# Column halves in one group, an earlier read of one result and fewer warm-up products in a Strassen-type matmul with GELU

## The chip, the core and the metric

The kernel runs on one core of a Trainium2 chip. The metric is the device time of a whole execution in microseconds (us), the median of several runs. "Before" is the kernel without the change, "after" the kernel with it. Every run told here was in the fast state, with a granted TensorE clock of 0.999 or 1.000, except for three runs of e_order: they count as fast too, but had 0.998, which is taken up there. "Span" is the time from the first to the last instruction of a profiled run.

The engines: PE is TensorE (matmuls), PEld its weight loads, DVE is VectorE (element-wise sums, transposes), ACT is ScalarE (copies, GELU, squares), POOL is GpSimd (it issues the loads of the inputs), SP issues the output transfers. PE writes its sums to a memory of its own, PSUM, which is divided into banks.

## The reference

```
a, b: 4096 x 4096, float32
x = a @ b
out = 0.5 * x * (1 + tanh(sqrt(2 / pi) * (x + 0.044715 * x**3)))     # float32
```

## The kernel before

The operands are turned to 16 bits on their way in. Each matrix is cut into four quadrants, and the four quadrants of the result come out of seven products instead of eight (M1 to M7, with sums of quadrants as operands). The result is worked through in 16 groups; a group is one block of 512 x 512 in each quadrant of the result. The first group's first half of K is done by plain products, while the inputs come in ("load phase"). All later groups have 7 products x 4 steps x 16 matmuls.

```python
PRODUCTS = [
    ("M3", "Y", "11", ("12", "22", 1)),           # name, PSUM chain, operand of a, operand of b
    ("M5", "X", ("11", "12", -1), "22"),
    ("M7", "X", ("12", "22", -1), ("21", "22", 1)),
    ("M1", "X", ("11", "22", -1), ("11", "22", -1)),
    ("M4", "X", "22", ("21", "11", 1)),
    ("M2", "Y", ("22", "21", -1), "11"),
    ("M6", "Y", ("21", "11", -1), ("11", "12", 1)),
]
N_WARM = 46
AHEAD = 2
```

The sums are made on DVE two steps ahead of their use (`make_sums`, tiles aS and bS, three buffers each). A step is 16 matmuls of 512 columns: four row blocks i, four pieces j of K.

```python
    def products(acc, sa, sb, i, start, stop):
        ...
        for j in range(4):
            nc.tensor.matmul(
                acc[:, :], sa[:, j // 2, i * P : (i + 1) * P, j % 2], sb[:, j, :],
                start=start and j == 0, stop=stop and j == 3, skip_group_check=True,
            )

    def multiply(gi, s, q):
        name, chain = product(gi, s)[:2]
        first = q == 0 and name in ("M3", "M5")
        sa, sb = sums.pop((gi, s, q))
        for i in range(RT):
            acc = bank(gi, chain, i) if first else banks[chain, i]
            products(acc, sa, sb, i, first, q == QPH - 1)
            if q == QPH - 1:
                settle(gi, name, i)
```

`settle` combines the banks of PSUM when a product is complete. The ends of M2 (result C21) and of M6 (result C22) matter here. Each y has one of five buffers, which is free again when its output transfer has landed:

```python
    def new_y():
        return pool.tile([P, NC], F32, name="y", tag="y", bufs=5)
    ...
        elif name == "M2":
            y = new_y()
            tt(y, post.pop(("x1", i)), Y, ALU.subtract)     # reads the bank that M6 goes on to write
            if gi:
                flush()
            waiting.append((gi, i, 1, 0, y, y))
        elif name == "M6":
            y = new_y()
            tt(y, Y, post.pop(("x7", i)), ALU.add)
            flush()                                         # GELU and output of what waits
            waiting.append((gi, i, 1, 1, y, y))
```

The order in which DVE gets its work is that of the program:

```python
        for n, step in enumerate(steps):
            for fn, args in before.get(n, ()):
                fn(*args)                                   # loads, transposes, squares of this step
            if n + AHEAD < len(steps):
                gi, s, q = steps[n + AHEAD]
                if s >= 0:
                    make_sums(gi, s, q)
            if step[:2] != (0, 2):
                flush()
            combine()
            if step[1] < 0:
                plain(n)
            else:
                multiply(*step)
            if step == (0, 2, QPH - 1):
                flush()
```

## Time and profile before

| | before |
|---|---|
| median (range) of three runs | 1580.12 us (1579.08 to 1580.46) |
| span of the profiled run | 1577.1 us |
| PE busy | 1567.7 us, 7246 matmuls |
| DVE busy | 1233.7 us |
| PE starts: the first real product; the product that waits for b's transfer; M6 of the first group; third step of the second group | 14.37, 35.74, 113.72, 128.23 us |

PE is busy for 99% of the span, so what can be gained without taking matmuls away is the handful of gaps in the rest. A gap is found in the list of waits, and where it lies is found in the order of time. Two cautions on reading. A matmul's duration in the records (379 ns) is its latency; the cost is the distance between starts (216 ns). And a gap in the order of time counts from the modelled end of the matmul before; where I give a wait to 0.01 us, it is the distance between the two starts in the trace's records less 0.216, and comes out 0.16 us larger.

### The profile page before, as it was taken

The numbers are of one execution on the slowest core, as the hardware profiler recorded it, in microseconds if no ns is written. First come the engines' busy times: TensorE is split into PE (matmuls) and PEld (weight loads), VectorE is DVE, ScalarE is ACT, GpSimd is POOL, SyncE is SP. The second block draws the span as 40 slices with busy tenths as digits, with TensorE's granted clock in tenths as the row PEclk, the third lists the DMA queues.
The fourth block names the chain that finished last, engine by engine and source line by source line (L and its number), as shares of the span: only waits on it lengthen the run. The fifth ranks groups of instructions, "written<-read, shape, count | busy, mean of one in ns | idle before, by whom it ended". The sixth has DMA issues, their size and how long they took to land. (4 is left out here: it accounts for less than half of the span.)

```text
span 1577.1 us, 19678 instructions
## 1 busy us (share of the span) xinstructions
PE 1567.7 (99%) x7246; PEld 709.6 (45%) x7246; DVE 1233.7 (78%) x1381; ACT 518.0 (33%) x710; POOL 537.7 (34%) x980
## 2 busy tenths in 40 slices
PE   9999999999999999999999999999999999999998
PEld 4444444444444444444444444444444444444443
DVE  1698888967787888895778778887687778988775
ACT  1036445311122545531111344542211145364111
POOL 7753442420234144341124413245011443314400
PEclk9999999999999999999999999999999999999999
DMA  9999884882968378686597937679468885747802
GB/s 173 198 215 189 132 162 79 161 162 48 193 106 158 87 131 160 108 179 115 87 161 117 186 72 142 146 113 182 79 121 146 134 160 93 151 105 134 161 28 82
DMA packets 225047, 211.13 MB, mean 134 GB/s; under 512 B 20144, under 2 KB 192176, under 8 KB 224944
## 3 DMA queue, kind: packets, MB, share of 16 engines
q0 software_dynamic: 187648, 142.67, 61.7%
q1 hardware_dynamic: 37296, 67.13, 11.8%
q8 instruction: 59, 0.97, 0.2%
q14 instruction: 44, 0.36, 0.1%
HBM read 285.22 MB, written 67.11 MB: 223 GB/s over the span
## 5 line engine op out<-in xcount | busy, mean ns | idle before, releaser
L331 PEld LDWEIGHTS <-aS 128*128 128x128 f16 x4960 | 485.3, 98 | 587.2 <-issue 2.2
L186 POOL DMA_DIRECT2D bR<-in_b_dram x832 | 447.6, 544 | 700.0 <-DVE bS L302 329.7
L302 DVE TENSOR_TENSOR aS<-aT 128x2048 f16<-128x2048 f16 (+1 forms) x312 | 376.1, 1212 | 151.0 <-PE accX L331 114.5
L331 PE MATMUL accX<-bS,aS 128*128 128x512 f16 x1984 | 431.1, 379 | 0.0
L302 DVE TENSOR_TENSOR bS<-bR 128x2048 f16<-128x2048 f16 x310 | 376.1, 1218 | 69.3 <-PE accX L331 58.5
L331 PEld LDWEIGHTS <-aT 128*128 128x128 f16 x1984 | 194.2, 98 | 234.8 <-issue 0.8
L422 ACT ACTIVATE y<-y 128x512 f32<-128x512 f32 x192 | 118.5, 630 | 351.8 <-DVE y L431 351.4
L331 PE MATMUL accY<-bS,aS 128*128 128x512 f16 x992 | 216.7, 379 | 1.8 <-DVE y L431 1.8
L331 PE MATMUL accY<-bS,aT 128*128 128x512 f16 x992 | 216.9, 379 | 0.5 <-DVE bS L302 0.5
L331 PE MATMUL accX<-bS,aT 128*128 128x512 f16 x992 | 216.7, 379 | 0.0
L331 PE MATMUL accX<-bR,aS 128*128 128x512 f16 x992 | 216.7, 379 | 0.0
L331 PE MATMUL accY<-bR,aS 128*128 128x512 f16 x992 | 216.7, 379 | 0.0
L186 POOL DMA_DIRECT2D stage<-in_a_dram x144 | 89.9, 630 | 249.0 <-DVE aT L161 178.0
L431 DVE TENSOR_TENSOR energy<-energy,square 128x1024 bf16<-128x1024 bf16 x240 | 164.4, 685 | 9.5 <-ACT square L207 5.7
L395 ACT COPY x<-accX 128x512 f32<-128x512 f32 x128 | 74.9, 585 | 224.3 <-PE accX L331 224.3
L207 ACT ACTIVATE square<-aT 128x1024 bf16<-128x1024 f16 x120 | 123.4, 1051 | 70.6 <-DVE energy L431 70.2
L207 ACT ACTIVATE square<-bR 128x1024 bf16<-128x1024 f16 x120 | 123.0, 1050 | 62.5 <-DVE energy L431 60.5
L161 DVE STREAM_TRANSPOSE aT<-stage 128x2048 uint32<-128x2048 uint32 (+1 forms) x37 | 74.6, 2017 | 46.0 <-DMA stage<-in_a_dram 39.9
L395 ACT COPY m<-accX 128x512 f32<-128x512 f32 x60 | 34.7, 579 | 215.7 <-PE accX L331 213.6
L422 ACT ACTIVATE y<-accX 128x512 f32<-128x512 f32 x64 | 38.2, 597 | 100.1 <-PE accX L331 99.9
L431 DVE TENSOR_TENSOR x<-accX,x 128x512 f32<-128x512 f32 x64 | 44.0, 691 | 21.8 <-ACT y L422 19.1
L431 DVE TENSOR_TENSOR y<-accY,m 128x512 f32<-128x512 f32 x60 | 39.9, 687 | 12.5 <-ACT m L395 12.4
(38 smaller groups left out, 344.9 us busy)
## 6 DMA issues: line engine op xcount, KB each, us to landing
bR<-in_b_dram POOLq DMA_DIRECT2D x832, 128.0 KB, 5.2
out_dram<-y SPq DMA_DIRECT2D x256, 256.0 KB, 5.7
stage<-in_a_dram POOLq DMA_DIRECT2D x112, 256.0 KB, 6.8
stage<-in_a_dram POOLq DMA_DIRECT2D x32, 128.0 KB, 5.1
row<-seen_d SPq DMA_DIRECT2D x2, 1.5 KB, 4.2
seen_d<-seen SPq DMA_DIRECT2D x1, 3.0 KB, 7.4
```

Of the source, the lines that this page charges most:

```text
L161: nc.vector.transpose(dst[:, :, x, :], src[:, :, x, :])
L186: nc.gpsimd.dma_start(out=dst, in_=src)
L207: nc.scalar.activation(t[:, :], src, ACT.Square)
L302: nc.vector.tensor_tensor(out=x, in0=y, in1=z, op=ALU.add if o[2] > 0 else ALU.subtract)
L331: nc.tensor.matmul(acc[:, :], sa[:, j // 2, i * P : (i + 1) * P, j % 2], sb[:, j, :], start=start and j == 0, stop=stop and j == 3, skip_g ...
L395: nc.scalar.copy(out=t[:, :], in_=src[:, :])
L422: nc.scalar.activation(y[:, :], src[:, :], ACT.Gelu_apprx_tanh)
L431: nc.vector.tensor_tensor(out=o[:, :], in0=x[:, :], in1=y[:, :], op=op)
```

## The change

Its intent, as far as the code tells: the third group (`gi == 2`) is multiplied in column halves; the reads of C21 go ahead of M6's last operand sums on DVE, so that M6 need not wait for its banks; and seven warm-up products that only keep the clock up go.

```diff
--- before.py
+++ after.py
@@ -49,7 +49,7 @@
     ("22", "21", "12", True), ("22", "22", "22", True),
 ]
 N_PLAIN = 2 * len(PLAIN)
-N_WARM = 46
+N_WARM = 39
 
 
 SQUARE_MAX = 2.0**26
@@ -323,15 +323,17 @@
         banks[chain, i] = t
         return t
 
-    def products(acc, sa, sb, i, start, stop):
+    def products(acc, sa, sb, i, start, stop, parts=1):
 
         sa = sa.rearrange("p (jj m e) -> p jj m e", jj=2, e=2)
         sb = sb.rearrange("p (kt n) -> p kt n", n=NC)
-        for j in range(4):
-            nc.tensor.matmul(
-                acc[:, :], sa[:, j // 2, i * P : (i + 1) * P, j % 2], sb[:, j, :],
-                start=start and j == 0, stop=stop and j == 3, skip_group_check=True,
-            )
+        w = NC // parts
+        for n in range(0, NC, w):
+            for j in range(4):
+                nc.tensor.matmul(
+                    acc[:, n : n + w], sa[:, j // 2, i * P : (i + 1) * P, j % 2], sb[:, j, n : n + w],
+                    start=start and j == 0 and n == 0, stop=stop and j == 3, skip_group_check=True,
+                )
 
     def warm():
         z = pool.tile([P, NC], F16, name="zeros", tag="bS", bufs=AHEAD + 1)
@@ -386,7 +388,7 @@
         sa, sb = sums.pop((gi, s, q))
         for i in range(RT):
             acc = bank(gi, chain, i) if first else banks[chain, i]
-            products(acc, sa, sb, i, first, q == QPH - 1)
+            products(acc, sa, sb, i, first, q == QPH - 1, parts=1 + (gi == 2))
             if q == QPH - 1:
                 settle(gi, name, i)
 
@@ -577,6 +579,8 @@
     at(len(groups) - 1, 2, 2, answer)
     at(len(groups) - 1, 4, 0, read)
 
+    late = (0, NP - 1, QPH - 1)
+
     with tc.manual_schedule():
         warm()
         table = pool.tile([P, 1], F32, name="table", tag="table")
@@ -586,9 +590,9 @@
             for fn, args in before.get(n, ()):
                 fn(*args)
             if n + AHEAD < len(steps):
-                gi, s, q = steps[n + AHEAD]
-                if s >= 0:
-                    make_sums(gi, s, q)
+                ahead = steps[n + AHEAD]
+                if ahead[1] >= 0 and ahead != late:
+                    make_sums(*ahead)
             if step[:2] != (0, 2):
                 flush()
             combine()
@@ -598,6 +602,8 @@
                 multiply(*step)
             if step == (0, 2, QPH - 1):
                 flush()
+            if step == (0, NP - 2, QPH - 1):
+                make_sums(*late)
         flush()
     return said["value"]
```

## The prediction

> **What bounds the kernel now.** I read the page first, then the list of who waited for whom on the matmul engine, then the order of time around each of those waits.
>
> The page's share of busy time says that TensorE matters:
>
> ```profile
> PE 1567.7 (99%) x7246; PEld 709.6 (45%) x7246; DVE 1233.7 (78%) x1381; ACT 518.0 (33%) x710; POOL 537.7 (34%) x980
> ...
> L331 PE MATMUL accX<-bS,aS 128*128 128x512 f16 x1984 | 431.1, 379 | 0.0
> ```
>
> The 379 ns is a latency, not the cost: 1984 matmuls kept the engine busy for 431.1 us, about 217 ns each. The windows view gives the rate without the ramp (columns: stretch, its length, busy time and count, clock, DMA share, GB/s); the second line is the third group:
>
> ```profile
> 218.00:314.50 96.50, 96.50 (x449) 1.00 0.70 131
> 320.00:1500.00 1180.00, 1180.00 (x5469) 1.00 0.72 131
> ```
>
> 1180 / 5469 = 215.8 ns per matmul, at full clock with no gap (record by record the starts are 215 or 216 ns apart). A weight load takes 98 ns (the mean in the page's row of L331 LDWEIGHTS) and starts 2 ns after the matmul ahead of it, so it is hidden with some 118 ns to spare. Everything that PE waits for after the warm-up is three waits:
>
> ```profile
> PE accY L331 <- DVE y L431: 1.8, 1, 1.8
> PE accX L343 <- DVE table L583: 1.4, 1, 1.4
> PE accY L331 <- DVE bS L302: 0.5, 1, 0.5
> PE accY L362 <- DMA bR<-in_b_dram: 0.5, 1, 0.5
> ```
>
> The second of these four is the program's start. From 128.23 us to the end PE runs 6688 matmuls without a gap, so any change of PE time after 128.23 arrives at the end in full, and any change before it arrives only if the matmul at 128.23 moves.
>
> **What the Trainium skill says.** Four places bear on it.
> - TensorE: Matmul & The Clock Gate, section "Wait — 56ns, not 53.3ns?": back-to-back warm matmuls start N / 2.4 GHz plus about 2.5 ns apart, a fixed cost per matmul. For 512 columns that is 215.8, which is what the trace has. For 256 it gives 109.2 ns; no row here shows that width yet.
> - The same page, "Back-to-back issue gap": in streams of weight load and matmul, 128 columns sustained about 81 ns per pair. So a pair can go faster than 109. The same sentence gives 131 ns for 512 columns, which this trace contradicts.
> - The same page, "What's actually happening": the clock is halved after at least one idle window of about 3.4 us. The trace agrees at the start: matmuls 427 ns apart until 7.4 us, then 216; and the waits of up to 1.9 us later did not lower the clock.
> - Trainium Kernel Development and Optimization, "Key Constraints": transfers issued from SP, ACT and POOL run on the same 16 DMA engines and interleave. The trace agrees: around 118 us an output of 256 KB takes 5.4 us to land behind loads.
>
> **Part 1, the third group by halves.** The group has 28 steps of 16 matmuls, 448 of 512 columns. The change makes them 896 of 256 columns, each with its own weight load: the column loop is outside, so the same four weights are loaded twice. The columns streamed stay the same, so with the rate formula the cost is the fixed part alone: 448 x 2.5 = +1.1 us (448 x 215.8 = 96.7 us becomes 896 x 109.2 = 97.8 us). The room for the weight load shrinks from 118 ns to 109 - 100 = 9 ns, by the trace's own 98 ns and 2 ns offset. That still fits, and the 81 ns pair says that the real limit is lower. The group has no wait of PE on anything, and DVE was busy 83.3 of 96.5 us there, so a slightly slower PE meets no new wait. It is on the path in full.
>
> **Part 2, C21's sums.** In the first group M2 finishes C21's base in the Y banks, and M6 adds on to the same banks, so DVE must read each bank (y = x - accY) before M6 may write it. DVE's order was: M6's four operand sums, then the four reads. The PE rows, and the DVE rows behind them:
>
> ```profile
> 104.88 7.07 PE L331 MATMUL accY<-bR,aS 128*128 128x512 f16 x32
> 113.72 7.07 PE L331 MATMUL accY<-bS,aS 128*128 128x512 f16 x32 [1.77 <-DVE y L431]
> ```
> ```profile
> 110.72 1.22 DVE L302 TENSOR_TENSOR aS<-aT 128x2048 f16<-128x2048 f16 x1
> 111.85 1.22 DVE L302 TENSOR_TENSOR bS<-bR 128x2048 f16<-128x2048 f16 x1
> 112.99 2.48 DVE L431 TENSOR_TENSOR y<-x,accY 128x512 f32<-128x512 f32 x4
> 115.38 1.22 DVE L302 TENSOR_TENSOR bS<-bR 128x2048 f16<-128x2048 f16 x1
> 116.51 2.49 DVE L431 TENSOR_TENSOR y<-y,c 128x512 f32<-128x512 f32 x4
> 118.92 1.22 DVE L302 TENSOR_TENSOR bS<-bR 128x2048 f16<-128x2048 f16 x1
> 120.06 0.68 DVE L431 TENSOR_TENSOR y<-accY,x 128x512 f32<-128x512 f32 x1
> 123.45 0.69 DVE L431 TENSOR_TENSOR y<-accY,x 128x512 f32<-128x512 f32 x1 [2.71 <-DMA out_dram<-y]
> 124.81 0.69 DVE L431 TENSOR_TENSOR y<-accY,x 128x512 f32<-128x512 f32 x1 [0.67 <-ACT y L422]
> 126.36 0.69 DVE L431 TENSOR_TENSOR y<-accY,x 128x512 f32<-128x512 f32 x1 [0.85 <-DMA out_dram<-y]
> 126.96 1.22 DVE L302 TENSOR_TENSOR bS<-bR 128x2048 f16<-128x2048 f16 x1
> ```
>
> The change swaps the first two rows with the third. The reads then start at 110.72 and are through by 113.2; M6 can follow M2 at 111.79 (111.57, the start of M2's last matmul, plus 0.216). M6's second step is due 16 x 0.216 = 3.45 us later, at 115.24, and needs the sum that now ends at about 114.24 + 1.22 = 115.46. PE's starts trail such an end by 0.05 us here, so it begins at 115.51: a new wait of 0.27. M6 ends 16 matmuls later, at 118.96 instead of 120.62: 1.66 us earlier.
>
> But the four DVE instructions only change places. DVE had been busy without a break since before 108, so the row at 115.38 and all after it stay where they are. The next group's third step needs the sum at 126.96, which stands in DVE's queue behind four writes of y. Those wait for buffers of y, five in all, which come free when C21's own outputs have landed. Outputs are issued when the sums with c (116.51) and their activations are done, and these don't move. So the sum still ends at 128.18 and the matmul still starts at 128.23. PE now arrives at 118.96 + 2 x 3.45 = 125.87 and waits 2.36 us instead of 0.70. Waits before: 1.93 + 0.70 = 2.63 (2.147 and 0.917 between starts, less 0.216 each; the view has 1.77 and 0.54, which count a modelled end). After: 0.27 + 2.36 = 2.63. Net **0**.
>
> **Part 3, 39 warm products.** Seven warm matmuls less are 7 x 0.216 = 1.5 us of PE work, ending at 14.30 - 1.51 = 12.79 instead of 14.30. But the first real matmul needs its transposed tile (DVE, first half done at 13.0) and its piece of b, whose last transfer landed at 14.24; the weight load started at 14.34. It was data that set that time, not the warm products. Even if it moved, PE is stopped further on by a transfer that nothing in PE releases:
>
> ```profile
> 14.37 7.07 PE L362 MATMUL accY<-bR,aT 128*128 128x512 f16 x32
> ...
> 35.74 1.45 PE L362 MATMUL accY<-bR,aT 128*128 128x512 f16 x6 [0.49 <-DMA bR<-in_b_dram]
> ```
>
> So the idle time before the data grows by 1.5 us and the end gets nothing: **0**. The sum of the three parts is +1.1 us, 1580.1 + 1.1 = 1581.2.
>
> **Rivals.**
> 1. The M6 gain is kept. That needs the y buffers to come free earlier, which would take earlier landings of C21's outputs. Against it: their issue hangs on DVE's fixed order, and DMA is saturated there. If all of the 1.66 came through: 1581.2 - 1.7 = 1579.5.
> 2. Weight loads become the bound of the halves. For it: only 9 ns to spare by the 98 ns of the profile. The TensorE page's "Step-by-step: what each phase is for" also has about 62 ns per matmul in the sequencer with hardware decode off; if a weight load costs the same, a pair takes 124 ns, an estimate from that page. Then 896 x 124 = 111.1 us, +14.4, giving 1594.5. Fully serial, 109 + 98 = 207 ns a pair, it would be 185 us, +89. Against both: weight loads now start right after a matmul's start and are hidden, and the page's 81 ns pair.
> 3. A longer idle stretch drops the clock: 2.36 us at 125.87 or 1.5 us before 14.3. Below 3.4 us, so I don't expect it; one window at half clock costs at most 1.7 us, and in the start the transfer at 35.74 hides most of it.
>
> **Range and chances.** Runs of before lie within 1.4 us. I take 1578.6 as the low end (rival 1 with noise) and 1585.5 as the high end (a pair of 109.2 + 5 ns would add 4.5 us). Slower by 2% needs +31.6 us, that is 143 ns a pair; faster by 2% cannot come from under 3 us of waits. I give 0.01, 0.97 and 0.02.
>
> **What would show it.** In the changed profile: the third group's matmuls as 896 rows in about 97.8 us, starts 109 ns apart; M6 starting near 111.8; a wait of some 2.4 us on DVE's bS sum just before 128.2, and 2.6 us of waits in that region as before; the first real matmul still near 14.4 and the wait near 35.7 unchanged. It is wrong if starts in the third group are well above 110 ns, or if the matmul after the bS sum begins before 127.5.

## The result, and the profile after

| | before | after |
|---|---|---|
| median (range), 4 runs each | 1579.91 us (1579.08 to 1580.46) | 1580.11 us (1579.39 to 1580.56) |
| span of the profiled run | 1577.1 | 1578.4 |
| first real product | 14.37 | 13.95 |
| wait for b's transfer ends | 35.74 | 35.34 |
| M2 starts | 104.88 | 105.89 |
| M6 starts | 113.72 | 112.80 |
| third step of the next group starts | 128.23 | 128.25 |
| third group, from its first start to the next group's | 96.7 (448 x 215.8 ns) | 97.81 (896 matmuls) |
| start of the last matmul | 1571.50 | 1572.64 |

The ratio of after to before is 1.0002, 95% interval 0.9987 to 1.0017: the same. A ratio here is the mean time of one kernel's fast runs over that of the other's of the same rounds, so it is not quite the ratio of the medians that are quoted beside it. The predicted 1581.2 (+1.1 us) lies inside the interval, and so does no change at all; the times alone don't tell those apart, the traces and the experiments do. In the two traces the third step of the second group starts 0.02 us later than before and the last matmul 1.13 us later: the +1.1 lies behind 128.25.

From the page of after: the busy time and the largest group of matmuls. Its mean of 366 ns mixes the two widths.

```profile
PE 1566.9 (99%) x7687; PEld 752.4 (48%) x7687; DVE 1233.5 (78%) x1381; ACT 518.3 (33%) x710; POOL 539.3 (34%) x980
...
L333 PE MATMUL accX<-bS,aS 128*128 128x512 f16 (+1 forms) x2112 | 431.6, 366 | 1.1 <-DVE aS L302 0.7
```

There are 441 matmuls more (448 by the halves, less 7 warm ones), and PE is busy for 0.8 us less: the warm products' 1.5 us are gone, and 0.7 came again, by the halves for the most part (in the trace of the halves alone PE is busy for 0.3 us more than before, not 1.1: these sums of modelled ends are too coarse for a count). The windows view of after over the third group (stretch, its length, busy time and count, clock, DMA share, GB/s):

```profile
218.10:315.70 97.60, 97.60 (x896) 1.00 0.70 131
```

97.60 / 896 = 108.9 ns; by the records the starts are 109.17 ns apart and the group lasts 97.81 us. I had written 109.2 and 97.8.

All waits of PE in after (engine, what it was to do, whom it waited for; total us, times, longest):

```profile
PE accY L364 <- DMA bR<-in_b_dram: 2.3, 2, 1.8
PE accX L345 <- DVE table L587: 1.4, 1, 1.4
PE accY L333 <- DVE bS L302: 1.3, 2, 0.7
PE accX L333 <- DVE aS L302: 0.7, 1, 0.7
PE accX L333 <- ACT m L397: 0.4, 1, 0.4
```

The 1.8 us wait for y at M6 is gone. In its place there are a wait for data at the start, two for bS and two new ones for aS and m. Their places, from the order of time of after's PE (start, length, what, count, and the gap before it with who ended it), the start first:

```profile
13.95 7.07 PE L364 MATMUL accY<-bR,aT 128*128 128x512 f16 x32 [1.75 <-DMA bR<-in_b_dram]
```

```profile
35.34 7.07 PE L364 MATMUL accY<-bR,aT 128*128 128x512 f16 x32 [0.51 <-DMA bR<-in_b_dram]
...
85.03 1.47 PE L333 MATMUL accX<-bS,aS 128*128 128x512 f16 x6 [0.69 <-DVE aS L302]
86.90 12.25 PE L333 MATMUL accX<-bS,aS 128*128 128x512 f16 x56 [0.41 <-ACT m L397]
...
112.80 3.62 PE L333 MATMUL accY<-bS,aS 128*128 128x512 f16 x16
117.04 3.61 PE L333 MATMUL accY<-bS,aS 128*128 128x512 f16 x16 [0.63 <-DVE bS L302]
120.49 7.07 PE L333 MATMUL accY<-bS,aT 128*128 128x512 f16 x32
128.25 7.07 PE L333 MATMUL accY<-bS,aT 128*128 128x512 f16 x32 [0.68 <-DVE bS L302]
```

M6 starts right behind M2 (105.89 + 6.91 = 112.80), as the change wants. Its second half then waits, and two steps later PE waits again and starts where it did before. The waits at 85 and 87 us belong to the load phase: a piece of a landed later in this run, and they lie ahead of the first DVE instruction that the change moves. DVE behind M6, in after's order of time:

```profile
111.73 1.87 DVE L433 TENSOR_TENSOR y<-x,accY 128x512 f32<-128x512 f32 x3
114.03 0.69 DVE L433 TENSOR_TENSOR y<-x,accY 128x512 f32<-128x512 f32 x1 [0.43 <-DMA out_dram<-y]
114.64 1.22 DVE L302 TENSOR_TENSOR aS<-aT 128x2048 f16<-128x2048 f16 x1
115.77 2.35 DVE L302 TENSOR_TENSOR bS<-bR 128x2048 f16<-128x2048 f16 x2
...
126.37 0.69 DVE L433 TENSOR_TENSOR y<-accY,x 128x512 f32<-128x512 f32 x1 [1.01 <-DMA out_dram<-y]
126.98 1.21 DVE L302 TENSOR_TENSOR bS<-bR 128x2048 f16<-128x2048 f16 x1
```

The reads of C21 now stand first; the fourth meets a y buffer whose output has not landed (0.43 us). The last line is the sum that the third step of the next group waits for. It still stands behind the writes of y, and they still wait for output transfers. (The same rows of before are in the prediction.)

### The profile page after: what moved, and what is told of

It reads as the page before. It is cut to its first block, busy times and chain, and to the rows that moved or that the text cites. A ratio compares the mean times of both kernels' runs of the same rounds, so it can differ in the third digit from the quotient of the medians.

```text
span 1578.4 us, 20560 instructions
## 1 busy us (share of the span) xinstructions
PE 1566.9 (99%) x7687; PEld 752.4 (48%) x7687; DVE 1233.5 (78%) x1381; ACT 518.3 (33%) x710; POOL 539.3 (34%) x980
## 5 line engine op out<-in xcount | busy, mean ns | idle before, releaser
L333 PEld LDWEIGHTS <-aS 128*128 128x128 f16 x5280 | 516.6, 98 | 557.0 <-issue 1.6
L333 PE MATMUL accX<-bS,aS 128*128 128x512 f16 (+1 forms) x2112 | 431.6, 366 | 1.1 <-DVE aS L302 0.7
L333 PEld LDWEIGHTS <-aT 128*128 128x128 f16 x2112 | 206.7, 98 | 222.7 <-issue 1.0
L333 PE MATMUL accY<-bS,aT 128*128 128x512 f16 (+1 forms) x1056 | 217.0, 366 | 0.7 <-DVE bS L302 0.7
L333 PE MATMUL accY<-bS,aS 128*128 128x512 f16 (+1 forms) x1056 | 217.0, 366 | 0.6 <-DVE bS L302 0.6
L333 PE MATMUL accX<-bR,aS 128*128 128x512 f16 (+1 forms) x1056 | 216.9, 366 | 0.0
L333 PE MATMUL accX<-bS,aT 128*128 128x512 f16 (+1 forms) x1056 | 216.9, 366 | 0.0
L333 PE MATMUL accY<-bR,aS 128*128 128x512 f16 (+1 forms) x1056 | 216.9, 366 | 0.0
```

The costliest lines, as they stand in the source:

```text
L333: nc.tensor.matmul(acc[:, n : n + w], sa[:, j // 2, i * P : (i + 1) * P, j % 2], sb[:, j, n : n + w], start=start and j == 0 and n == 0, s ...
```

## The experiments

Each run is of its own kernel, beside runs of before on the same chip. The single runs of before ranged over 1577.27 to 1580.82 us in these sets, so a difference of 1 us is at the edge of what the times can tell, and I use the traces for it.

**The halves alone (e_half).** The change of `products` and its call as in the diff above, with 46 warm products and the old order.

> The third group's halves alone, 46 warm products, old order of sums. Theory (a fixed 2.5 ns per matmul, weight loads hidden, all of it behind the last wait of the matmul engine): the group takes 97.8 us instead of 96.7, and the end comes 1.1 us later; ratio about 1.0007. Rival (the changed kernel's halves are free or the front part gave something back, since its median moved by only 0.2 us): 0 to 0.3 us.

Measured: 1580.22 us median (1579.42 to 1580.97) beside 1579.13, ratio 1.0006, interval 0.9992 to 1.0019. In the trace the group lasts 97.81 us, starts 109.17 ns apart, no wait in it. The centre fits +1.1 us; the interval does not exclude the rival, so the next run makes the cost larger.

**The halves in fifteen groups (e_half_all).**

```diff
-            products(acc, sa, sb, i, first, q == QPH - 1, parts=1 + (gi == 2))
+            products(acc, sa, sb, i, first, q == QPH - 1, parts=1 + (gi > 0))
```

> Halves in all fifteen groups after the first, nothing else changed: the suspected cost fifteen times over. Theory: 15 x 448 x 2.5 ns = 16.8 us more, about 1596.8 us, ratio 1.0106, matmul starts 109.2 ns apart throughout. Rival (the small difference seen is noise and the halves cost nothing): ratio 1.000. Rival (halves burden weight loads or fetching of instructions when they go on for long): over 25 us.

Measured: 1595.5 us (1594.54 to 1596.42) beside 1579.13, ratio 1.0100, interval 1.0085 to 1.0115; 16.4 us by the medians, 1.09 us a group. The windows view of this run over the same long stretch as in the prediction:

```profile
320.00:1500.00 1180.00, 1180.00 (x10812) 1.00 0.72 131
```

1180 / 10812 = 109.1 ns, against 215.8 for a matmul of double width: 2 x 109.1 - 215.8 = 2.4 ns for each matmul more. The cost of the halves is settled: it is a fixed cost per matmul (a third width follows in the next run), it is on the path in full, and it does not grow over fifteen groups.

**Quarters in the third group (e_quarter).** This asks how near the halves were to the limit of weight loads. "The skill's 81 ns" is the figure of "Back-to-back issue gap" that the prediction names.

```diff
+            products(acc, sa, sb, i, first, q == QPH - 1, parts=1 + 3 * (gi == 2))
```

> Third group by column quarters of 128, 1792 matmuls and weight loads. It asks how much room the halves had. If only the fixed cost counts, 1792 x 55.8 ns = 100.0 us, 3.3 us more than before. If a weight load must end before its matmul (2 + 98 ns): 1792 x 100 = 179 us, 82 us more. With the skill's 81 ns a pair: 145 us, 48 us more. I expect the 81 ns, so about 1628 us; the halves' 109 would then have 28 ns to spare.

Measured: 1582.12 us (1581.84 to 1583.49) beside 1579.13, ratio 1.0017, interval 1.0001 to 1.0032. I expected about 1628 and was wrong. The third group in the windows view of this run:

```profile
219.10:318.90 99.80, 99.80 (x1790) 1.00 0.69 129
```

99.80 / 1790 = 55.8 ns a pair, with a weight load for every matmul. The group lasted 100.0 us by the records, 3.3 more than before, which is the fixed cost alone. The records of weight loads still say 98 ns each, and nearly every one starts 1 to 2 ns after the matmul ahead of it, so here their records overlap one another: 98 ns is a latency too. The 9 ns of room that I gave the halves, and the 28 ns, were both no measure of it.

**88 warm products (e_warm88).** `N_WARM = 88`, nothing else.

> 88 warm products instead of 46, nothing else changed: 42 x 0.216 = 9.07 us more work of the matmul engine before its first real product. Theory (three waits in the first group soak up a shift of the start): they have 0.65 + 1.93 + 0.70 = 3.3 us to give, so the end comes 5.8 us later, and those three waits are gone from the trace. Rival (the start is on the path): 9.1 us later. Rival (transfers released later by the shift put new waits in their place): over 7 us.

Measured: 1585.97 us (1585.75 to 1586.49) beside 1579.13, ratio 1.0041, interval 1.0026 to 1.0057: 6.8 us by the medians, between the theory and the first rival. The wait for b's transfer is gone from the trace, as expected. The other two are not:

```profile
121.52 7.07 PE L331 MATMUL accY<-bS,aS 128*128 128x512 f16 x32 [1.42 <-DVE y L431]
...
136.01 7.07 PE L331 MATMUL accY<-bS,aT 128*128 128x512 f16 x32 [0.52 <-DVE bS L302]
```

Both moved with PE (M6 from 113.72 to 121.52, the third step from 128.23 to 136.01). They are not fixed points in time: DVE is fed by PE, and when all of it is late the wait is late too. Only the wait at 35.7, which is for a transfer that PE does not release, soaks up a shift of the start. By this trace the first real product started 8.88 us later (23.25 against 14.37); 8.88 - 0.65 (that wait) - 0.08 (a small one of before at 85.9) - 0.37 (what the other two shrank by) = 7.78, and both the third step and the end of the span come 7.8 later than in before's profiled run. Why the medians give a microsecond less is not shown; other runs of before in this set were not traced.

**39 warm products alone (e_warm39).** `N_WARM = 39`.

> 39 warm products alone. Theory (data sets the start of the first real product, and the later waits soak up the rest): 0, within 0.3 us, the first real product still between 13.9 and 14.4 us. Rival (the start moves and reaches the end): up to 1.5 us faster. Rival (the gap before the first product brings the clock down): about 1 us slower or hidden by the waits.

Measured: 1578.36 us (1577.97 to 1579.01) beside 1578.96, ratio 0.9997, interval 0.9983 to 1.0010. The first rival at its full 1.5 us (0.9990) is inside the interval, so the trace must say: the first real product started at 13.19, outside what I expected, and the wait near 35 ended at 34.90. Starting 1.2 us earlier than before's profiled run went with 0.8 there. But runs with 46 warm products had this wait end anywhere from 34.71 to 36.61, and the clock stayed up (starts 216 ns apart from the first real product on). I read it as no effect that can be told from the spread of the loads; a gain of some tenths of a microsecond is not excluded. One thing the traces do show against the theory: in five of the nine traced runs with 46 warm products (e_half, e_quarter, e_order_b, e_first, e_defer) the first real product started 0.216 us after the last warm one, with no wait between them (13.50 to 14.26 us). There the warm products and not the data set its start.

**One warm product (e_warm0).** `N_WARM = 1`.

> One warm product instead of 46. Theory: the first real product starts at about 14 us as before, since data sets it, but at half clock: up to 16 matmuls 427 ns apart instead of 216, 3.4 us later at most. The wait for b's transfer near 35.7 gives back 0.65 us (up to 1.2 in a late run); the waits after it don't, as the run with 88 warm products showed. So 1.5 to 2.8 us slower, ratio 1.001 to 1.0018. Rival (the matmul engine has time to spare in the load phase): 0.

Measured: 1579.38 us (1579.09 to 1579.61) beside 1579.03, ratio 1.0002, interval 0.9987 to 1.0018. I expected 1.5 to 2.8 us and got 0.3. Only ten real products started 427 ns apart (the start of before has 14 such distances; with a distance of 381 ahead of them and one of 277 behind, 2.1 us were lost, not 3.4), the first started at 13.28 instead of 14, and no wait is left near 36: the products that wait there in the other runs start at 36.12, which is inside the range of those runs. In the profiled run the third step came at 129.23, 1.0 us later than in before's. So even 45 warm products less cost too little to tell from the spread by the times, and from 7 less I expect no more.

**The order of C21's sums alone (e_order, and again as e_order_b).**

```diff
-                if s >= 0:
+                if s >= 0 and (gi, s, q) != (0, 6, 3):
                     make_sums(gi, s, q)
...
+            if step == (0, 5, QPH - 1):
+                make_sums(0, 6, QPH - 1)
```

> The order of C21's sums alone. Theory (the matmul engine only arrives earlier at its next wait, the sum of the next group's third step, which stands behind four writes of y that wait for buffers): 0, within 0.4 us; the wait just before 128 us grows to about 2.4 us, unless the transfers of this run put it elsewhere. Rival (the 1.7 us gained at M6 reach the end): 1.7 us faster, ratio 0.9989.

Measured: 1580.74 us (1579.13 to 1581.05) beside 1578.96, ratio 1.0010, interval 0.9996 to 1.0024. The rival's 0.9989 is excluded. From the order of time of this run's PE:

```profile
112.45 7.35 PE L331 MATMUL accY<-bS,aS 128*128 128x512 f16 x32
119.63 7.07 PE L331 MATMUL accY<-bS,aT 128*128 128x512 f16 x32
128.61 7.07 PE L331 MATMUL accY<-bS,aT 128*128 128x512 f16 x32 [1.91 <-DVE bS L302]
```

M6 has 0.28 us of wait left inside it (0.27 predicted), and PE then waits 2.07 for the third sum instead of 0.70. The time itself looked slower (1.8 us by the medians, where I expected at most 0.4), so I ran the same kernel again.

> The same kernel as e_order, a second time, because its first timing (ratio 1.0010, interval 0.9996 to 1.0024) left open whether the order of C21's sums costs something of its own. Theory (it is worth nothing either way, and the first set was the spread of the load phase): a ratio within 0.9994 to 1.0006. Rival (reading C21 earlier meets output buffers that have not landed, and costs about 1 us): again 1.0005 to 1.0015. The waits before its third step should again sum to about 2.4 us from M6 on.

Measured: 1579.01 us (1578.32 to 1581.03) beside 1579.03, ratio 1.0005, interval 0.9992 to 1.0019. Here the loads came early (35.7 is 34.71 in this run), PE ran ahead, and the wait for the third sum was 3.15 us; with 0.27 in M6 that is 3.42 us, not the 2.4 that I expected. Neither set shows a cost or a gain clear of noise, and 1.0005 lies in the range of the theory and at the edge of the rival's.

What the two sets do show is two clusters: 1578.32 to 1579.13 us (four runs, both traced ones among them) and 1580.29 to 1581.05 (six runs). Three of the slower six, all of e_order, had a granted clock of 0.998. In all 13 traces kept, the clock, once up, was at half only behind the last matmul and for at most 3.0 us, which makes 0.999 of the span (1 - 0.5 x 3.0 / 1577 = 0.99905). To be shown as 0.998 it takes at least 0.0015 x 1577 / 0.5 = 4.7 us at half clock, so in these three runs the clock was very likely down somewhere else too. The longest stretch without a matmul behind the start is the one before the third step (3.36 us from start to start in e_order_b), so the prediction's rival 3 may hold there: a longer wait that brings the clock down, worth up to 1.7 us by its estimate. That is not shown: none of the slower six was traced, three of them had 0.999, and runs of before with 1.000 reach 1580.82 too. No run of after had under 0.999.

The sharper measure of the waits is the distance in the trace from M2's first matmul to the third step's first, which leaves the load phase out (without any wait it would be the two steps of M2, the two of M6 and two more, 6 x 3.45 = 20.7; all columns in us, the waits from the distances of starts):

| kernel | near 35.7 | M2 starts | waits in M6 | wait, 3rd step | M2 to 3rd step |
|---|---|---|---|---|---|
| before | 35.74 | 104.88 | 1.93 | 0.70 | 23.35 |
| e_half | 35.20 | 104.45 | 1.93 | 0.84 | 23.49 |
| e_warm39 | 34.90 | 104.08 | 1.93 | 0.87 | 23.52 |
| e_warm0 | 36.12 | 105.19 | 1.58 | 1.75 | 24.04 |
| e_warm88 | 43.97 | 113.03 | 1.58 | 0.68 | 22.98 |
| after | 35.34 | 105.89 | 0.79 | 0.85 | 22.35 |
| e_order | 35.25 | 105.54 | 0.28 | 2.07 | 23.07 |
| e_order_b | 34.71 | 103.87 | 0.27 | 3.15 | 24.14 |
| e_first | 34.94 | 104.20 | 1.94 | 0 | 22.66 |
| e_order_first | 36.18 | 105.24 | 0 | 0 (4th: 1.36) | 20.73 |
| e_defer | 35.45 | 104.80 | 0.27 | 0 | 20.99 |

With the old order of everything the last column is 22.98 to 24.04 (first five rows), with C21's reads moved and nothing else in the queue 22.35 to 24.14 (after, e_order, e_order_b). The order moves the wait; what it does to the sum is within the spread between runs of one kernel (23.07 and 24.14 for e_order). The last three rows are of the runs that follow.

**The third sum first (e_first).** The old order of C21's reads, but the sum for the third step of the next group is put ahead of the four writes of y.

```diff
             products(acc, sa, sb, i, first, q == QPH - 1)
-            if q == QPH - 1:
+            if q == QPH - 1 and (gi, name) != (0, "M6"):
                 settle(gi, name, i)
+        if q == QPH - 1 and (gi, name) == (0, "M6"):
+            make_sums(1, 0, 2)
+            for i in range(RT):
+                settle(gi, name, i)
...
-                if s >= 0:
+                if s >= 0 and (gi, s, q) != (1, 0, 2):
```

> Old order of C21's sums, but the sum of the next group's third step is issued ahead of the four writes of y that wait for buffers. Theory: that takes away the last wait, 0.7 us faster, and the wait at M6 stays 1.9 us. Rival (the sum is late for its operands or its buffer, not for its place in the queue): 0.

Measured: 1577.43 us (1577.12 to 1577.93) beside 1578.96, ratio 0.9990, interval 0.9976 to 1.0004; unclear by the times alone. In the trace the wait before the third step is gone, and the one at M6 is 1.94 as before. So the sum was late for its place in the queue, not for its operands or its buffer: it now starts at 120.15 us instead of 126.96.

**Both orders (e_order_first).** The edits of the last two together.

> Both: the changed order of C21's sums, and the next group's third sum ahead of the writes of y; no halves, 46 warm products. Theory (the two waits are in series and each alone hides the other's gain): up to 2.3 us faster than before, about 1577.7, with 0.3 us left of the waits at M6 and in the next group together; somewhat less in a run whose loads come late. Rival (DMA sets the pace up to here and puts the wait at another transfer): under 0.7 us.

Measured: 1577.07 us (1576.27 to 1578.85) beside 1578.96, ratio 0.9985, interval 0.9971 to 0.9999. By the times this is not clear of the sum alone (0.9990). By the traces, from M2's first matmul to the fourth step's, it takes 25.5 us here (20.73 + 3.45 + 1.36), 26.1 in e_first and 25.8, 26.5 and 27.6 in the three traces with the new order of C21's reads and the old place of the third sum (after, e_order, e_order_b). So both edits together gain little more than one, in the profiled run at least, which was the slowest of the five:

```profile
119.06 10.52 PE L331 MATMUL accY<-bS,aT 128*128 128x512 f16 x48
130.77 3.61 PE L331 MATMUL accY<-bS,aT 128*128 128x512 f16 x16 [1.19 <-DVE bS L302]
```

Three steps now run through (x48), and the fourth waits: its sum is the next one behind the same four writes of y.

**C22's writes put off (e_defer).** The new order of C21's reads, and the four writes of y after the next group's second step, so that both sums stand ahead of them.

```diff
             products(acc, sa, sb, i, first, q == QPH - 1)
-            if q == QPH - 1:
+            if q == QPH - 1 and (gi, name) == (0, "M6"):
+                held.append(acc)
+            elif q == QPH - 1:
                 settle(gi, name, i)
...
+            if step == (1, 0, 1):
+                for i, acc in enumerate(held):
+                    y = new_y()
+                    tt(y, acc, post.pop(("x7", i)), ALU.add)
+                    flush()
+                    waiting.append((0, i, 1, 1, y, y))
```

> The changed order of C21's sums, and the four writes of C22's y put off until after the next group's second step, so that both remaining sums of M3 (third and fourth step) stand ahead of them in the vector engine's queue. Theory (in e_order_first the wait only moved from the third sum to the fourth): M6's second half waits 0.3 us, the third and fourth steps wait for nothing, and the end comes about 2.3 us earlier than before, ratio 0.9985 or less, and less than e_order_first's wait of 1.2 us at the fourth step. Rival (the squares and later sums then come late instead): a new wait of 1 us or more between 130 and 150 us.

Measured: 1576.42 us (1575.11 to 1577.80) beside 1579.03, ratio 0.9983, interval 0.9969 to 0.9996. All waits of PE in this run:

```profile
PE accX L343 <- DVE table L587: 1.4, 1, 1.4
PE accY L362 <- DMA bR<-in_b_dram: 0.6, 1, 0.6
PE accY L331 <- DVE bS L302: 0.3, 1, 0.3
```

The waits between M2 and the next group's end are down to 0.27 us, which hides in M6's rows; the 0.3 in the last line lies at 1183 us, where a sum stands behind a transpose that waited for its load. Before, PE reached that place just as its sum was ready (1184.95 against 1184.90), so a front part that is still faster would meet this wait next. This version beats before by 2.6 us in the medians of the same set, clear of noise. Its median is also below that of after (1576.42 against 1580.11), but those two were not timed in the same rounds, so that difference is not measured.

## Why the prediction was right

By its own steps:

- **What bounds the kernel.** PE without a gap after 128.23 us held: the halves' cost, placed behind it, came out at the end in full (fifteen times over, 16.4 us for 16.8). "Any change before it arrives only if the matmul at 128.23 moves" held too: it started at 128.25 in after. That the two figures are so close is partly chance. M2 began 1.0 us later in this run, C21's outputs were issued from 119.47 on instead of 117.93, but the first three still landed at about the same times (the third at 126.25 and 126.23), and the writes of y wait for these.
- **Part 1, +1.1 us.** Right in mechanism and size: 97.81 us for 97.8, 109.17 ns for 109.2. The fixed cost per matmul of the Trainium skill (TensorE: Matmul & The Clock Gate, "Wait — 56ns, not 53.3ns?") is what the runs show at three widths: 215.8, 109.2 and 55.8 ns. What was wrong is the argument on room: 98 ns is no bound, as the quarters showed (the room before was also 116 by its own 2 + 98 ns, not 118), so rival 2 had even less for it than I thought.
- **Part 2, net 0.** Right. M6 followed M2 without a wait, and the gain was lost at the next group's third sum, by its place behind the writes of y (shown by the three runs that changed that place). Two sizes were off in after's own trace: the wait in M6's second half was 0.79 us, not 0.27, because the fourth read of C21, now earlier, met a y buffer still in flight; and the wait at the third step was 0.85, not 2.36, because PE was 1.0 us late from the load phase and lost those 0.5. Together that is 1.64 us of waits, not the 2.6 that the prediction named as its sign; the 1.0 that is missing went into M2's later start. In the runs with the order alone they were 0.28 and 0.27, and 2.07 and 3.15. The step that did not hold as worded is that all rows of DVE "stay where they are": they stay in their order, and move with PE and the loads by about a microsecond from run to run.
- **Part 3, 0.** Nothing contradicts it, but no run shows it to better than the spread of the loads. In after PE stood idle for 1.91 us before 13.95 until data came, and the next gate (a wait that the change does not move) ended at 35.34. "It was data that set that time, not the warm products" holds for the profiled runs of before (by 0.07 us) and after; in five other runs with 46 warm products it did not, and what remains of the argument is the gate. The clock did not drop in after (rival 3): behind the stretch of 1.91 us, as behind that of 3.15 us in e_order_b, the next starts are 216 ns apart. For three runs of e_order it is open.
- **The measured +0.2** is less than +1.1 by 0.9 us, and that the median came so near is no evidence for the parts. The span of the profiled run is 1.3 us longer; the interval of the times covers both. What the runs leave open is only this remainder, which is smaller than the spread that the load phase gives to single runs.

## What to carry to other kernels

When an in-order engine makes the bottleneck wait, moving its instructions about can just move the wait to the next one that stands behind the same slow thing: here four writes that waited for output buffers. Find that thing and take the urgent work out from behind it; here the gain at M6 then came through (23.35 us before, 20.99 in e_defer, in the last column of the table). And before giving a saving in the front of a kernel any credit, look for the next gate that it does not move.

## What the Trainium skill lacked or had wrong

- TensorE: Matmul & The Clock Gate, "Back-to-back issue gap": it has 81 ns per pair of weight load and matmul at 128 columns and 131 ns at 512. The runs show 55.8 ns at 128 (1790 pairs), 109.2 at 256 and 215.8 at 512, each with a weight load for every matmul, so the formula that the page calls the isolated gap is the one that fits these streams.
- The same page, "LDWEIGHTS (loading the stationary operand)": it gives P / 1.2, 106.7 ns for 128 columns. The records have 98 ns (151 while the clock was down), and pairs 55.8 ns apart show that neither is what a load adds to a stream here.
- No page that I read has what an output costs a buffer when loads share the DMA engines: 256 KB landed 5.4 to 7.9 us after issue around 118 to 128 us of before, and 2.0 us at 149 us, after the loads had ended.
